# A zero-padded rotary key and regrouped SSD output products in a hybrid encoder layer on one Trainium2 core

## The chip, the cores and the metric

The kernel runs on 1 core of one Trainium2 chip. The metric is the device time of one execution in microseconds (us). Three runs of the kernel before gave a median of 2013.43 us (2013.3 to 2013.7). Below, PE is the matrix engine (TensorE) and PEld its weight load, DVE is VectorE, ACT is ScalarE, SP is the engine that issues most transfers.

## What is computed

The reference is one layer of a bidirectional encoder, 256 tokens of 2048 channels, float32 throughout:

```
n   = RMSNorm(h)
u   = n @ W_in        # MLA latents, rope key | SSD z, xBC, dt | gates
a   = MLA(u_mla)      # scores = q_nope.k_nope + q_rope.k_rope, softmax, @ v
s   = BiSSD(u_ssd)    # Mamba-2 SSD, two chunks of 128 tokens, both directions
m   = sigmoid(g_a) * a + sigmoid(g_s) * s
h   = h + m @ W_out
h   = h + ConvGatedMLP(RMSNorm(h))
out = RMSNorm_final(h)
```

Two places matter here. In the attention, 16 heads each have 128 plain channels and 64 rotary channels; the rotary key is one for all heads, so a head's scores are a product over 128 channels plus one over 64. In the SSD, 8 groups of 8 heads (64 channels a head) produce y = (own chunk's product) + (the other chunk's state, times a decay) + d * x.

## The kernel before, in words

**Precision.** Nearly every operand of a large product is split into a high part (rounded to float32r) and a low part (what is left), and a product is taken as high x high + high x low + low x high. The parts of the weights are made on the fly: `split_to` (L133) takes half a slab of 16 blocks from `raw`, ACT makes `wh` (L139) and DVE makes `wl` (L140). Five such halves are kept (HB=5), so a half that PE has finished makes room for the half five places later.

**Jobs and slots.** The work is a list of jobs, one slab of weights [128, 16 x 128] each. A job that is not merged does 48 products of 256 columns (`mm3`, L144 to L147), a merged one 16 of 512 and 16 of 256 columns (L165, L166). A job's place in the list is its slot. Work beside the weights is put into slots with `at(slot, function)` (L899) and is issued ahead of the job of that slot; a compiler's scheduler then orders each engine's instructions by that priority and by when their inputs are expected to be ready. Inside a slot PE does the side work in the order in which it is written.

**Attention.** `kr_evac` and `kr_rope` (L444 to L454, slot 14) make the rotary key once: its 64 rotated channels lie twice in 128 rows, and `krH` and `krL` are the high and the low part of all 128 rows. A rotary query `rp` (L456 to L488) has, for each head, its high part in one half of the 128 rows and its low part in the other half. `att1` (L536) makes the scores of one head, for two blocks `c` of 128 queries: three products of the plain channels, one product of `rp` with all rows of `krH` (L546, high x high and low x high at once), and one product of the 64 rows of `rp` that hold its high part with the same 64 rows of `krL` (L547). Then come the softmax on DVE and ACT (L549 to L557), transposes on PE (`att2`, L565) one slot later, and the product with the values (`att3`) another slot later. There is one `att1` for each of the 16 heads.

**SSD.** A group is 11 or 12 jobs. `ssd_xt` (L697) transposes x, `ssd_y` (L710) makes the output products, `ssd_fin` (L735) applies the gate and sums squares. `ssd_y(g, j0)` handles two of the group's four blocks `j` of 128 channels. For each block it does the products from the other chunk (L720, 128x128 weights, float32, two products that take two instructions each) and then the own chunk's products (L725, 128x64 weights, four products of two instructions, alternating between output rows 0 to 63 and 64 to 127). It is called at slot e for j0 = 0 and at slot e + 1 for j0 = 2, where e is the first slot of the next group (L1011, L1012). DVE then does L728, L731 (twice) and L733 for each call.

PSUM for side work is a pool of four banks (`spsum`, L79); each call of `ssd_y` takes two of them, `ssd_xt` two, `ssd_cb` one. Pages of SBUF come from one pool of 29 (`page`, L70), smaller tiles from one of 18 (`p1`, L73).

```
        at(b + 8 + f, ssd_xt, g)
        at(b + e, ssd_y, g, 0)
        at(b + e + 1, ssd_y, g, 2)
        at(b + e + 2, ssd_fin, g, 0)
        at(b + e + 3, ssd_fin, g, 2)
```

Of the kernel before, what the change touches and what calls it, by code (L numbers as in the profile page):

```python
# [9 lines left out]
F32R = mybir.dt.float32r  # L10
# [15 lines left out]
# columns of the packed per-channel vectors: [128, n] each  # L26
# [7 lines left out]
# columns of the shape-only constants  # L34
# [3 lines left out]
# 2 pi and the parts of a turn that 2^12 and 2^22 radians leave, as parts whose products are exact  # L38
# and a last one
# [4 lines left out]
# blocks of the SSD gate's columns of w_in that go between each group's (x and z, after z)  # L44
# [3 lines left out]
class Job:  # L48
    """One pass of a slab of weights [128, nb * 128] over the tensor engine."""
# [8 lines left out]
def tile_bidir_hybrid_layer(ctx: ExitStack, tc, xT, pos, vec, cst, w_in, w_r, w_v, w_qk, w_oa,  # L58
# [26 lines left out]
    # ---- inputs that everything needs  # L85
# [21 lines left out]
    # ---- the stream of weights: raw (DMA) -> high part (ACT) -> low part (DVE)  # L107
# [4 lines left out]
    def load(i):  # L112
        if i >= len(jobs) or i in raws:
            return
        j = jobs[i]
        t = wp.tile([P, 16, P], F32, tag="raw", bufs=RAWB, name="raw")
        raws[i] = t
        if i == 0:
            # the first slab comes in halves, between the pieces of x
            for h in range(2):  # L120
                load_x(2 * h)
                nc.sync.dma_start(t[:, 8 * h:8 * h + 8, :], j.src[:, 8 * h:8 * h + 8, :])
                load_x(2 * h + 1)
        elif i == 1:
            for h in range(2):
                nc.sync.dma_start(t[:, 8 * h:8 * h + 8, :], j.src[:, 8 * h:8 * h + 8, :])
        else:
            nc.sync.dma_start(t[:, :j.nb, :], j.src)
# [20 lines left out]
    def dense(src, nb, get, evac, cell=None, k0=0, ktot=None, merge=True):  # L149
        """One block of 128 output channels; get(k) -> [128, 2, 256], high and low activations.  # L150

        With merge, the two products of the high weights are one matmul of 512 columns, and the
        block comes as two halves that evac adds up."""
        cell = {} if cell is None else cell
        ktot = nb if ktot is None else ktot

        def mm(h, n, wh, wl):
            if k0 == 0 and h == 0:
                cell["ps"] = gpsum([P, 2, S] if merge else [P, S])
            ps = cell["ps"]  # L160
            for b in range(n):
                k = k0 + 8 * h + b
                x = get(k)
                if merge:
                    pe.matmul(ps, lhsT=wh[:, b, :], rhs=x, start=k == 0, stop=False)  # L165
                    pe.matmul(ps[:, 0, :], lhsT=wl[:, b, :], rhs=x[:, 0, :], start=False, stop=k == ktot - 1)  # L166
                else:
                    mm3(ps, wh[:, b, :], wl[:, b, :], x[:, 0, :], x[:, 1, :], k == 0, k == ktot - 1)

        def ev():  # L170
            if k0 + nb == ktot:
                evac(cell["ps"])
        j = Job(src, nb, mm, ev)
        jobs.append(j)
        return j
# [12 lines left out]
    def token_sums(accs):  # L188
        """Sums over the channels of what is in accs, one token a partition: two [128, 1] in PSUM."""
        ss = [spsum([P, 1]), spsum([P, 1])]  # L190
        for i, a in enumerate(accs):
            for c in range(2):
                pe.matmul(ss[c], lhsT=a[:, c * P:(c + 1) * P], rhs=ones[:, :1], start=i == 0,
                          stop=i == len(accs) - 1)
        return ss
# [8 lines left out]
    def spread(r):  # L204
        """[128 tokens, 2] -> [128, 256] in PSUM: the token's value on every partition."""
        dg = p1((P, 2, P), name="dg")
        ps = spsum([P, S])
        for c in range(2):
            dve.tensor_scalar(dg[:, c, :], ident, r[:, c:c + 1], None, ALU.mult)
            pe.matmul(ps[:, c * P:(c + 1) * P], lhsT=ones, rhs=dg[:, c, :], start=True, stop=True)  # L210
        return ps
# [7 lines left out]
    # ---- n = RMSNorm(x), split. The latents, which are normalised themselves, start from x * w.  # L219
# [41 lines left out]
    # ---- rotary tables  # L261
    rot = {}

    def rope_tables():
        """A step of one instruction at a time."""
# [23 lines left out]
        # angle = a + 2^12 q + 2^22 qh, all three exact; the last two as a part t of a turn  # L289
# [23 lines left out]
    def swapped(q, nb):  # L313
        """q with the two halves of 32 channels of every head swapped."""
        sw = page([P, nb, S], name="sw")
        for i in range(4):
            o = 32 * (i ^ 1)
            nc.scalar.dma_start(sw[o:o + 32], q[32 * i:32 * i + 32])
        return sw

    def rotate(q, sw, nb):
        """q, sw [128, nb, 256]: blocks of two heads of 64 channels; the rotated ones end up in q."""
# [4 lines left out]
    # ---- latents  # L327
# [14 lines left out]
    def lat_norm(which):  # L342
        # the latent is r_x * t: its mean square is r_x^2 * mean(t^2)
# [21 lines left out]
    # ---- dt, decays  # L365
# [45 lines left out]
    def dt_cumsum():  # L411
# [3 lines left out]
        for c in range(2):  # L415
            pe.matmul(ps[:, c, :64], lhsT=U, rhs=at[:, c, :64], start=True, stop=True)
            pe.matmul(ps[:, c, 64:], lhsT=L, rhs=at[:, c, 64:], start=True, stop=True)
            # the sum over the chunk that the other one is reached through
# [21 lines left out]
    # ---- MLA  # L440
# [8 lines left out]
    def kr_rope():  # L449
        t, sw = dts["krf"]  # L450
        rotate(t, sw, 1)
        kr[0], kr[1] = p1(dt=F32R, name="krH"), p1(dt=F32R, name="krL")
        act.activation(kr[0], t[:, 0, :], AF.Copy)
        dve.tensor_sub(kr[1], t[:, 0, :], f32(kr[0]))  # L454

    def r_job(i):  # L456
# [17 lines left out]
        def ro():  # L474
            for h in range(2):
                q, sw = cell["f", h]
                rotate(q, sw, 2)
                # a head's high and low parts, stacked: [high; low] for the first of a block's
                # two heads, [low; high] for the second
# [56 lines left out]
    def att1(h):  # L536
# [3 lines left out]
        rb, ro = (h // 2) % 2, 64 * (h % 2)  # L540
        ps = spsum([P, 2, S])
        for c in range(2):
            cs = slice(c * P, (c + 1) * P)
            mm3(ps[:, c, :], q[:, 0, b, cs], q[:, 1, b, cs], k[:, 0, b, :], k[:, 1, b, :], True, False)
            # the rotated key lies twice in kr: one matmul takes its high part with both parts of q
            pe.matmul(ps[:, c, :], lhsT=r[:, b, rb, cs], rhs=kr[0], start=False, stop=False)  # L546
            pe.matmul(ps[:, c, :], lhsT=r[ro:ro + 64, b, rb, cs], rhs=kr[1][ro:ro + 64, :], start=False, stop=True)  # L547
# [36 lines left out]
    # gates as tanh(u / 2); sigmoid(u) * y = (tanh(u / 2) + 1) * y / 2, the half comes with w_out  # L584
# [23 lines left out]
    # ---- SSD  # L608
# [46 lines left out]
    def ssd_decay(g, c):  # L655
# [4 lines left out]
        # decay from the chunk's edge, two heads of 64 channels a block  # L660
# [49 lines left out]
    def ssd_y(g, j0):  # L710
        q = grp[g]
        if j0 == 0:
            ypg[g] = page([P, 4, S], name="y")
        px, ps = spsum([P, 2, S]), spsum([P, 2, S])
        for b in range(2):
            j = j0 + b
            js = slice(j * P, (j + 1) * P)
            for c in range(2):
                # from the other chunk: forward into chunk 1, backward into chunk 0
                pe.matmul(px[:, b, c * P:(c + 1) * P], lhsT=q.xw[:, 1 - c, js], rhs=q.cX[:, 1 - c, :],  # L720
                          start=True, stop=True)
            for c in range(2):
                for hh in range(2):
                    h = 2 * j + hh
                    pe.matmul(ps[64 * hh:64 * hh + 64, b, c * P:(c + 1) * P],  # L725
                              lhsT=q.xt[:, c, h * 64:h * 64 + 64], rhs=q.F[c][:, h, :], start=True, stop=True)
        t = page([P, 2, S], name="yx")
        dve.tensor_mul(t, px, q.pr[:, j0:j0 + 2, :])  # L728
        y = ypg[g][:, j0:j0 + 2, :]
        for b in range(2):  # L730
            dve.scalar_tensor_tensor(y[:, b, :], q.x[:, j0 + b, :], vcol("dsk", 4 * g + j0 + b), ps[:, b, :],  # L731
                                     ALU.mult, ALU.add)
        dve.tensor_add(y, y, t)  # L733
# [54 lines left out]
    # ---- h = x + mixed @ w_out  # L788
# [34 lines left out]
    # ---- FFN  # L823
# [33 lines left out]
    def dn_evac(m, last):  # L857
        def ev(ps):
# [6 lines left out]
            if last:  # L865
# [5 lines left out]
                if m == 2:  # L871
                    # brings in the table that the last norm takes its root from
# [16 lines left out]
    # ---- the order of the work  # L889
# [7 lines left out]
    late = []          # (slot, function): work beside the slabs, in the slot in which it is issued  # L897
# [39 lines left out]
    # closures that look at state (lat) when they run, so build these jobs lazily  # L937
# [53 lines left out]
    for g in range(G):  # L991
# [19 lines left out]
        at(b + e, ssd_y, g, 0)  # L1011
        at(b + e + 1, ssd_y, g, 2)  # L1012
# [34 lines left out]
    # ---- run it  # L1047
# [4 lines left out]
    # the first slab goes through the tensor engine as float32: it needs no parts of its operands  # L1052
# [16 lines left out]
    # the tensor engine's clock comes up while the first data is on its way  # L1069
# [39 lines left out]
def _blocks(w, cols):  # L1109
    """[K, N] -> [len(cols) / 128, 128, K / 128, 128]: one contiguous slab per 128 columns."""  # L1110
# [5 lines left out]
def _layout(inp):  # L1116
# [39 lines left out]
    # rotary queries: [2, 128, block of 2 heads, k, 128]  # L1156
    a["w_r"] = uq[:, :, :, 128:].reshape(4, P, 2, 4, 128).transpose(2, 1, 3, 0, 4).reshape(2, P, 16, P)
    # values: [4, 128, k, 4 heads * 128]
    a["w_v"] = ukv[:, :, :, 128:].reshape(4, P, 4, 512).transpose(2, 1, 0, 3).reshape(4, P, 16, P)
    # per pair of heads: 2 blocks of queries, 2 of keys, [8, 128, block, k, 128]  # L1160
# [32 lines left out]
```

## Time and profile before

| | |
|---|---|
| Device time, median of 3 runs | 2013.43 us (2013.3 to 2013.7) |
| Span of the profiled execution, first to last instruction | 2011.6 us |
| The profiled execution's own time | not noted apart from the runs; 1.8 us lie between its span and the median |
| PE busy / PEld busy | 1997.7 us (99%) / 1813.1 us (90%) |
| DVE busy / ACT busy | 1477.0 us (73%) / 1187.5 us (59%) |
| Granted PE clock, mean | 0.998 of full speed |
| HBM, mean over the span | 187 GB/s |

The profile is of one execution. Matrix products are pipelined, so the duration of one (some 280 ns for 256 columns) overlaps the next; what a product costs in a stream is the step from its start to the next one's. The view of the chain that ended last gives these steps directly: each piece in it begins where the piece before it ends. Its PE times lie some 0.15 us behind those of the timeline.

### The profile page before, as it was taken

The numbers are of one execution on the slowest core, as the hardware profiler recorded it, in microseconds if no ns is written. First come the engines' busy times: TensorE is split into PE (matmuls) and PEld (weight loads), VectorE is DVE, ScalarE is ACT, GpSimd is POOL, SyncE is SP. The second block draws the span as 40 slices with busy tenths as digits, with TensorE's granted clock in tenths as the row PEclk, the third lists the DMA queues.
The fourth block names the chain that finished last, engine by engine and source line by source line (L and its number), as shares of the span: only waits on it lengthen the run. The fifth ranks groups of instructions, "written<-read, shape, count | busy, mean of one in ns | idle before, by whom it ended". The sixth has DMA issues, their size and how long they took to land.

```text
span 2011.6 us, 32781 instructions
## 1 busy us (share of the span) xinstructions
PE 1997.7 (99%) x13204; PEld 1813.1 (90%) x13204; DVE 1477.0 (73%) x2371; ACT 1187.5 (59%) x1880; POOL 0.2 (0%) x4
## 2 busy tenths in 40 slices
PE   9999999999999999999999999999999999999997
PEld 8988888999999999999888888888888888888886
DVE  7977656678778877877766666788756777567775
ACT  6655544677877877776644445655434555335564
POOL 0000000000000000000000000000000000000000
PEclk9999999999999999999999999999999999999999
DMA  7444345764556455554555555555555555555543
GB/s 273 173 170 142 130 156 207 252 215 167 193 207 224 160 203 210 176 199 174 189 203 201 201 215 194 183 192 192 185 183 187 187 189 188 188 187 183 184 164 121
DMA packets 58424, 379.54 MB, mean 189 GB/s; under 512 B 6816, under 2 KB 7456, under 8 KB 17568
## 3 DMA queue, kind: packets, MB, share of 16 engines
q1 hardware_dynamic: 56592, 375.08, 52.6%
q10 hardware_dynamic: 1680, 2.37, 0.4%
q8 instruction: 103, 1.69, 0.3%
q14 instruction: 49, 0.40, 0.1%
HBM read 371.91 MB, written 4.33 MB: 187 GB/s over the span
## 4 chain that ended last, share of the span: by engine, by line
PE 99%; DVE 1%; DMA 0%; ACT 0%; SPq 0%; DVEq 0%; issue 0%
PE g L165 41%; PE g L166 21%; PE g L145 10%; PE g L147 10%; PE g L146 10%; PE s L725 1%; PE s L720 1%; PE s L145 1%; PE s L547 0%; PE s L147 0%; PE s L146 0%; PE g L504 0%; PE g L506 0%; PE g L505 0%; PE s L704 0%; PE s L565 0%
## 5 line engine op out<-in xcount | busy, mean ns | idle before, releaser
L139 ACT ACTIVATE wh<-raw 128x1024 fp32r<-128x1024 f32 (+1 forms) x670 | 701.8, 1048 | 717.2 <-PE g L165 558.6
L140 DVE TENSOR_TENSOR wl<-raw,wh 128x1024 fp32r<-128x1024 f32 (+1 forms) x670 | 809.7, 1211 | 417.4 <-ACT wh L139 410.2
L165 PE MATMUL g<-hHL,wh 128*128 128x512 f32 x1360 | 477.6, 396 | 0.0
L145 PE MATMUL g<-xHL,wh 128*128 128x256 f32 x1424 | 405.6, 285 | 0.0
L147 PE MATMUL g<-xHL,wl 128*128 128x256 f32 x1424 | 403.1, 283 | 0.9 <-DVE wl L140 0.9
L146 PE MATMUL g<-xHL,wh 128*128 128x256 f32 x1424 | 403.0, 283 | 0.0
L166 PE MATMUL g<-hHL,wl 128*128 128x256 f32 x1360 | 381.7, 281 | 0.0
L165 PEld LDWEIGHTS g<-hHL,wh 128*128 128x128 f32 x1360 | 255.2, 188 | 60.7
L145 PEld LDWEIGHTS g<-xHL,wh 128*128 128x128 f32 x1424 | 272.3, 191 | 2.9 <-issue 2.2
L147 PEld LDWEIGHTS g<-xHL,wl 128*128 128x128 f32 x1424 | 272.3, 191 | 1.1 <-DVE wl L140 1.1
L146 PEld LDWEIGHTS g<-xHL,wh 128*128 128x128 f32 x1424 | 272.4, 191 | 0.1
L166 PEld LDWEIGHTS g<-hHL,wl 128*128 128x128 f32 x1360 | 257.1, 189 | 0.0
L165 PE MATMUL g<-aHL,wh 128*128 128x512 f32 x692 | 244.8, 399 | 0.0
L166 PE MATMUL g<-aHL,wl 128*128 128x256 f32 x692 | 193.9, 281 | 0.0
L165 PE MATMUL g<-xHL,wh 128*128 128x512 f32 x512 | 182.6, 400 | 0.0
L165 PE MATMUL g<-yHL,wh 128*128 128x512 f32 x480 | 166.5, 394 | 0.0
L165 PEld LDWEIGHTS g<-aHL,wh 128*128 128x128 f32 x692 | 130.1, 188 | 32.7 <-DVE aHL L849 0.6
L166 PE MATMUL g<-xHL,wl 128*128 128x256 f32 x512 | 143.5, 280 | 0.0
L166 PE MATMUL g<-yHL,wl 128*128 128x256 f32 x480 | 133.0, 277 | 0.0
L166 PEld LDWEIGHTS g<-aHL,wl 128*128 128x128 f32 x692 | 130.8, 189 | 0.1
L165 PEld LDWEIGHTS g<-xHL,wh 128*128 128x128 f32 x512 | 96.2, 188 | 23.4 <-issue 0.3
L165 PEld LDWEIGHTS g<-yHL,wh 128*128 128x128 f32 x480 | 90.1, 188 | 20.9
(295 smaller groups left out, 2742.4 us busy)
## 6 DMA issues: line engine op xcount, KB each, us to landing
raw<-in_w_in SPq DMA_DIRECT2D x120, 1024.0 KB, 4.8
raw<-in_w_up SPq DMA_DIRECT2D x88, 1024.0 KB, 4.8
raw<-in_w_os SPq DMA_DIRECT2D x32, 1024.0 KB, 4.8
raw<-in_w_dn SPq DMA_DIRECT2D x32, 1024.0 KB, 4.9
raw<-in_w_oa SPq DMA_DIRECT2D x16, 1024.0 KB, 4.8
FB<-acsD SPq DMA_DIRECT2D x32, 512.0 KB, 7.5
raw<-in_w_out SPq DMA_DIRECT2D x16, 1024.0 KB, 4.7
raw<-in_w_dn SPq DMA_DIRECT2D x16, 768.0 KB, 4.1
```

The lines of the kernel that those rows point to most:

```text
L139: act.activation(wh[:, :nb, :], r, AF.Copy)
L140: dve.tensor_sub(wl[:, :nb, :], r, f32(wh[:, :nb, :]))
L145: pe.matmul(ps, lhsT=wH, rhs=xH, start=first, stop=False)
L146: pe.matmul(ps, lhsT=wH, rhs=xL, start=False, stop=False)
L147: pe.matmul(ps, lhsT=wL, rhs=xH, start=False, stop=last)
L165: pe.matmul(ps, lhsT=wh[:, b, :], rhs=x, start=k == 0, stop=False)
L166: pe.matmul(ps[:, 0, :], lhsT=wl[:, b, :], rhs=x[:, 0, :], start=False, stop=k == ktot - 1)
L720: pe.matmul(px[:, b, c * P:(c + 1) * P], lhsT=q.xw[:, 1 - c, js], rhs=q.cX[:, 1 - c, :], start=True, stop=True)
L725: pe.matmul(ps[64 * hh:64 * hh + 64, b, c * P:(c + 1) * P], lhsT=q.xt[:, c, h * 64:h * 64 + 64], rhs=q.F[c][:, h, :], start=True, stop=True)
```

## The change

The rotary key's low part becomes two tiles, one for each head of a pair. In each, 64 rows hold the low part and the other 64 rows are zeros, so that the last product of a head's scores takes all 128 rows of `rp` and of the key. In the SSD, the two calls of `ssd_y` for a group become one call at slot e + 1, which issues the other chunk's products of the first two blocks, the own chunk's products of all four blocks, and the other chunk's products of the last two; the DVE work of both halves follows. Comments were taken out as well.

```diff
 def kr_rope():
     rotate(t, sw, 1)
-    kr[0], kr[1] = p1(dt=F32R, name="krH"), p1(dt=F32R, name="krL")
-    act.activation(kr[0], t[:, 0, :], AF.Copy)
-    dve.tensor_sub(kr[1], t[:, 0, :], f32(kr[0]))
+    kr["h"] = p1(dt=F32R, name="krH")
+    act.activation(kr["h"], t[:, 0, :], AF.Copy)
+    for b in range(2):
+        z = kr[b] = p1(dt=F32R, name="krL")
+        r, o = slice(64 * b, 64 * b + 64), slice(64 - 64 * b, 128 - 64 * b)
+        dve.memset(f32(z[o]), 0.0)
+        dve.tensor_sub(z[r], t[r, 0, :], f32(kr["h"][r]))
...
 def att1(h):
-    rb, ro = (h // 2) % 2, 64 * (h % 2)
+    rb = (h // 2) % 2
...
-        pe.matmul(ps[:, c, :], lhsT=r[:, b, rb, cs], rhs=kr[0], start=False, stop=False)
-        pe.matmul(ps[:, c, :], lhsT=r[ro:ro + 64, b, rb, cs], rhs=kr[1][ro:ro + 64, :], start=False, stop=True)
+        pe.matmul(ps[:, c, :], lhsT=r[:, b, rb, cs], rhs=kr["h"], start=False, stop=False)
+        pe.matmul(ps[:, c, :], lhsT=r[:, b, rb, cs], rhs=kr[b], start=False, stop=True)
...
-def ssd_y(g, j0):
+def ssd_y(g):
     q = grp[g]
-    if j0 == 0:
-        ypg[g] = page([P, 4, S], name="y")
-    px, ps = spsum([P, 2, S]), spsum([P, 2, S])
...
+    ypg[g] = page([P, 4, S], name="y")
+    px, ps = {}, {}
+    def cross(j0):
+        px[j0] = spsum([P, 2, S])
+        for b in range(2):
+            js = slice((j0 + b) * P, (j0 + b + 1) * P)
+            for c in range(2):
+                pe.matmul(px[j0][:, b, c * P:(c + 1) * P], lhsT=q.xw[:, 1 - c, js], rhs=q.cX[:, 1 - c, :],
+                          start=True, stop=True)
+    def own(j0):
+        ps[j0] = spsum([P, 2, S])
+        for b in range(2):
+            for c in range(2):
+                for hh in range(2):
+                    h = 2 * (j0 + b) + hh
+                    pe.matmul(ps[j0][64 * hh:64 * hh + 64, b, c * P:(c + 1) * P],
+                              lhsT=q.xt[:, c, h * 64:h * 64 + 64], rhs=q.F[c][:, h, :], start=True, stop=True)
+    cross(0)
+    own(0)
+    own(2)
+    cross(2)
+    for j0 in (0, 2):
+        t = page([P, 2, S], name="yx")
+        dve.tensor_mul(t, px[j0], q.pr[:, j0:j0 + 2, :])
         ...
...
-        at(b + e, ssd_y, g, 0)
-        at(b + e + 1, ssd_y, g, 2)
+        at(b + e + 1, ssd_y, g)
```

## Rows read from the trace of the kernel before

**Rows 1.** The profile's page: span, busy time, the chain that ended last

```profile
span 2011.6 us, 32781 instructions
...
PE 1997.7 (99%) x13204; PEld 1813.1 (90%) x13204; DVE 1477.0 (73%) x2371; ACT 1187.5 (59%) x1880; POOL 0.2 (0%) x4
...
PE 99%; DVE 1%; DMA 0%; ACT 0%; SPq 0%; DVEq 0%; issue 0%
```

**Rows 2.** PE's waits, longest in total first: us, times, longest

```profile
PE g L1056 <- DVE xw L225: 1.6, 3, 1.2
```

**Rows 3.** Groups by shape: PE in attention and SSD (busy, mean ns)

```profile
L547 PE MATMUL s<-krL,rp 64*128 64x256 f32 x32 | 12.2, 381 | 0.0
...
L725 PE MATMUL s<-FB,xt 128*64 128x128 f32 x256 | 21.1, 285 | 0.0
```

**Rows 4.** The chain that ended last, 116 to 119 us: start, us

```profile
116.96 0.12 PE s L546
117.08 0.31 PE s L547
117.39 0.31 PE s L145
117.71 0.12 PE s L146
```

**Rows 5.** The same chain around one call of ssd_y, 446 to 450 us

```profile
447.02 0.45 PE s L720 x4
447.47 0.59 PE s L725 x8
448.06 0.64 PE s L720 x4
448.70 0.59 PE s L725 x8
449.29 0.32 PE g L145
```

**Rows 6.** The same chain, single pieces inside that call

```profile
447.47 0.25 PE s L725
...
447.73 0.10 PE s L725
...
448.06 0.31 PE s L720
```

**Rows 7.** The same chain at a transpose of x, 434 to 436 us

```profile
434.63 0.88 PE s L704 x8
435.51 0.12 PE g L145
```

**Rows 8.** Line L546: its weight loads (duration ns min/median/max, first and last start)

```profile
L546 PEld LDWEIGHTS s<-krH,rp x32: 187/188/192, 116.7 to 259.9; 128*128 128x128 f32 x32
```

**Rows 9.** Timeline, 131 to 134 us: one head's softmax and its transposes

```profile
131.99 0.62 DVE L557 TENSOR_SCALAR p<-p,sm 128x256 f32<-128x256 f32 x2
...
132.73 0.60 PE L565 MATMUL s<-CT,p 128*128 128x128 f32 x4
```

**Rows 10.** Timeline, 103 to 106 us: the rotary key's low part and what follows

```profile
103.24 0.42 DVE L454 TENSOR_TENSOR krL<-krf,krH 128x256 fp32r<-128x256 f32 x1
103.58 2.35 DVE L140 TENSOR_TENSOR wl<-raw,wh 128x1024 fp32r<-128x1024 f32 x2
...
105.27 0.28 PE L147 MATMUL g<-latH,wl 128*128 128x256 f32 x1
```

**Rows 11.** Groups by shape: DVE's memset and its work for ssd_y

```profile
L731 DVE SCALAR_TENSOR_TENSOR y<-xs,V,s 128x256 f32<-128x256 f32 x32 | 14.4, 471 | 0.0
...
L728 DVE TENSOR_TENSOR yx<-s,pr 128x512 f32<-128x512 f32 x16 | 11.0, 686 | 1.0 <-PE s L720 0.6
...
L733 DVE TENSOR_TENSOR y<-y,yx 128x512 f32<-128x512 f32 x16 | 11.0, 686 | 0.2
...
L97 DVE MEMSET ones<- 128x128 f32 x1 | 0.2, 165 | 0.8 <-PEq L1182 0.8
```

**Rows 12.** ACT's longest wait, 400 to 960 us: us, times, longest

```profile
ACT wh L139 <- PE g L146: 94.1, 64, 2.2
```

More of the change, by code (lines that the diff above doesn't have):

```diff
@@ L708, in ssd_xt @@
                               wsuf[:, c, 8 * g:8 * g + 8].unsqueeze(2).broadcast_to([P, 8, 64]), ALU.mult)
-    def ssd_y(g, j0):
+    def ssd_y(g):
         q = grp[g]
-        if j0 == 0:
-            ypg[g] = page([P, 4, S], name="y")
-        px, ps = spsum([P, 2, S]), spsum([P, 2, S])
[L715 to L733, printed above, removed]
@@ L735, in ssd_fin @@
+        cross(0)
[5 more added lines that the diff above has]
+            dve.tensor_mul(t, px[j0], q.pr[:, j0:j0 + 2, :])
+            y = ypg[g][:, j0:j0 + 2, :]
+            for b in range(2):
+                dve.scalar_tensor_tensor(y[:, b, :], q.x[:, j0 + b, :], vcol("dsk", 4 * g + j0 + b),
+                                         ps[j0][:, b, :], ALU.mult, ALU.add)
+            dve.tensor_add(y, y, t)
     def ssd_fin(g, j0):
```

## The prediction

> **What bounds the kernel now.** I read the page first. PE is busy for 99% of the span, and the chain of work that ended last is 99% PE [rows 1]. PE's own list of waits confirms it: the largest of its five entries is 1.6 us, at the start of the kernel [rows 2]. So a microsecond taken from PE's stream comes off the end, unless something else becomes late. A busy PE hides how long a product really takes, since durations overlap (the 32 products of L547 average 381 ns [rows 3]), so I went to the chain, where each piece is a step in PE's stream. There the reader sees what the change is about. Products of one shape follow each other at 0.12 us for 256 columns. The 64-row product takes a step of 0.31, and so does the full product behind it, after which the step is 0.12 again [rows 4]. The same shows around the 64-column products of the SSD [rows 5, 6].
>
> **The padded key (attention).** Per block of queries the 64-row product costs 0.31 - 0.12 = 0.19 us more than its full twin L546 one row above, and the product after it another 0.31 - 0.12 = 0.19 [rows 4]. Padding adds no product and no column: the same 256 columns run through 128 rows, behind a product of the same shape, with the same stationary operand. I take 0.12 for it and 0.12 for the next. The group has 32 such products [rows 3], 16 heads of two blocks, and each is followed by a full-height product (the next block's or the next job's). Saved: 32 x 0.38 = **12.2 us**. As for bounds, the new product can hardly step below 0.12, the step of its twin; if it kept its 0.31 and only the return got free, 6.1 us would be saved. I take the upper end, since the row of the twin is an exact match in shape, columns and type.
>
> A rule speaks against padding. In the rows the 64-row product runs alone, and no other product shares its step [rows 4]. The Trainium skill, TensorEngine Tiling (Array Packing), section Theoretical Speedup, says that a contraction of 64 or less can run two to the array, up to twice as fast, which padding forgoes. By that price, estimated as half of a 0.12 step each, padding would cost 32 x 0.06 = 1.9 us where I count a gain. Nothing in this trace runs so, since both products of a head use the same 64 rows.
>
> **The key's preparation.** `kr_rope` loses one subtract of 128 rows (a 0.34 us step on DVE, 103.24 to 103.58 [rows 10]) and gets two of 64 rows and two memsets of 64 rows x 256. No row shows these. If half the rows cost half, the subtracts add nothing; if rows are free, they add 0.34. A memset of 128x128 took 0.165 us [rows 11]; twice the columns give at most 0.33. So 0.3 to 1.0 us more on DVE, once. Behind it in DVE's queue is the low part of the next half slab, ready near 103.58 + 1.2 = 104.8 (half of the 2.35 for two), and PE needs it at 105.27 [rows 10]. The cover is 0.5 us, so PE waits between 0 (or the memsets, which depend on nothing, go earlier) and 0.5. I take **0.3 us lost**. The half after that has another 2.9 us, 24 products at 0.12.
>
> **The SSD products.** Before, each of a group's four blocks goes 128x128, 128x64 and back. Entering: the first pair of 64-column instructions (two output halves side by side) takes 0.25, later pairs start 0.11 apart (0.25 + 3 x 0.11 makes the 0.59), so entering costs 0.14 [rows 5, 6]. Returning: the first L720 after it takes 0.31, against 0.45 / 4 = 0.11 in the call's first four; a dense product takes 0.32 against 0.12 [rows 5]. That is 0.20 either way, and 0.34 for entering and returning. After, a group does this once instead of four times: 3 x 0.34 x 8 groups = **8.2 us saved**. Adding the whole block up instead: before 2 x (0.45 + 0.59 + 0.64 + 0.59 + 0.20) = 4.94 us a group; after 0.90 for eight full ones, 0.25 + 15 x 0.11 for the 32 small ones, 0.31 + 7 x 0.11 for the last eight, 3.88. That gives 1.06 x 8 = 8.5, so the term is good to 0.3.
>
> Two steps inside the new block are not in the trace. A float32 product of full shape now stands right before the float32r dense ones; the nearest row, the float32 transposes of L704, shows no charge for that (0.12 behind them [rows 7]), the far one is the 0.20 above, so 0 to 1.6 us in all; I take 0. And the small products go from one PSUM bank to the next in mid-stream: 0 to 0.14 each, 1.1 us in all; I take 0, as pairs already alternate between output halves freely.
>
> **What is moved.** The j0 = 0 half goes one slot later, past the next group's first decay work on ACT and DVE. It issues no DMA; nothing on SP's or POOL's queue changes place. Its eight full and sixteen small instructions stay on PE. On DVE, two sets of 0.69 + 2 x 0.47 + 0.69 = 2.3 us (added durations) now come together, 4.6 us [rows 11]. Queued behind them are low parts of weights. Their cover: through the SSD, ACT waits for PE to free a weight buffer [rows 12], so the five halves are full; four halves of 24 x 0.12 = 2.9 us lie between, 11.5 us, less some 2.4 for the two splits of the refill, leaving 9. The burst fits twice. The block takes all four PSUM banks; their former users finished three slots earlier and the next one comes three slots later, at about 5.8 us a slot. `ssd_fin` of the first half now waits for the later block, but its sums are wanted only after the last group.
>
> A faster attention could make the softmax late. The closest head ends its scaling at 131.99 + 0.62 = 132.61, and PE transposes it at 132.73 [rows 9], 0.1 us of slack. But the PE work between that head's scores and its transposes is dense and untouched, so both sides move together; I charge nothing and keep 1 to 2 us for the range.
>
> **Sum.** 2011.6 - 12.2 - 8.2 + 0.3 = 1991.5 us of span [rows 1]. The profiled execution's own time is not noted apart; with the 1.8 us by which its span lies under the median of the runs, 2013.4 - 20.1 = **1993.3 us**. With the three unknown steps at their far ends it is 1996.2; with no stall and 8.5 for the SSD 1992.7. Scheduling shifts either way make this case's own range 1991.5 to 1996.
>
> **Rivals.** *The grouping does not come about.* The order on PE comes from a scheduler; if it puts dense products or the crossing ones between the small ones, the SSD term goes: 2013.4 - 12.2 + 0.3 = 2001.5. For: one more thing must be ready at once, four banks. Against: in rows 5 PE follows the code exactly, and so it does in all 16 calls in the chain. Chance 0.07.
>
> *The new product's weight load shows.* A load takes 0.188 us [rows 8], longer than a 0.12 step, so it is already under the product before it. If the padded one could not load under its twin, its step would be about 0.19 + 0.11 = 0.30, and only the return is saved, 32 x 0.19 = 6.1: 2013.4 - 6.1 - 8.2 + 0.3 = 1999.4. Against: L546 itself, a full-height load behind full-height products, steps at 0.12 [rows 4]. Chance 0.03. The Trainium skill, TensorE: Matmul & The Clock Gate, section The mechanism, says that a load overlaps running products only when its row group differs, which would give this case; the trace disagrees, by that 0.12.
>
> *The queues shift.* With new timings a softmax exponent or a page of SBUF lands behind something that waits for PE, for 0.3 us or so in some 16 heads and 8 groups: 3 to 10 us back, 1996 to 2003. For: the 0.1 us slack [rows 9] and the second `yx` page held at once. Chance 0.07.
>
> *Slower.* The DVE burst reaches PE: low parts of weights queue behind 4.6 us of output work in each group. It decides once PE stands over 20.1 / 8 = 2.5 us per group; with no lead at all it would be 8 x 4.6 = 36.8, or 2030 us. Against: the 9 us lead. Chance 0.03.
>
> **How the numbers follow.** The forecast case has 0.80. The range 1991 to 1998.5 holds it nearly whole and the near part of the queue case. A measurement of this kernel tells 0.2%, 4 us, from no change. All cases but the last are faster by more than that, save a corner of the queue case: faster 0.96, same 0.01, slower 0.03.
>
> **What would show it.** Right: in the chain the last product of `att1` and the one behind it step 0.12; a group's SSD block is one piece of 8, 32 and 8 instructions of about 3.9 us, with one 0.25 and one 0.31 in it and 0.12 behind it; PE's list of waits grows by less than 1 us; L547's group has the 128x128 shape. Wrong: L547 still at 0.3, several entries into the 128x64 shape per group, or PE waiting for `wl`, `p` or a PSUM bank in the middle of the kernel.

## The result and the profile after

The changed kernel took 1994.13 us (median of 4 runs, 1992.78 to 1994.73) against 2013.37 us: ratio 0.9906, 95% interval 0.9894 to 0.9918. The forecast was 1993.3 us. In a second comparison it took 1993.54 us (5 runs, 1992.60 to 1993.90) against 2013.14, ratio 0.9903 (0.9889 to 0.9917). The profiled execution is the slowest of the first four, 1994.73 us with a span of 1992.9, so 18.7 us of span are gone in it.

The page after, the same parts as in [rows 1]:

```profile
span 1992.9 us, 32794 instructions
...
PE 1979.4 (99%) x13204; PEld 1810.8 (91%) x13204; DVE 1471.3 (74%) x2374; ACT 1205.5 (60%) x1894; POOL 0.2 (0%) x4
...
PE 97%; DVE 2%; DMA 0%; ACT 0%; issue 0%; ACTq 0%; SPq 0%; DVEq 0%
```

PE is still busy for 99%, with the same 13204 instructions, so the gain is not work left out. The chain that ended last is 97% PE and no longer 99%: at one wait of PE near 106 us, explained below, it is followed back through DVE. The groups by shape (compare [rows 3]) show the low part's product at 128x128; L727 and L736 are now the lines of the crossing and the own products:

```profile
L727 PE MATMUL s<-cX,xw 128*128 128x128 f32 x128 | 17.7, 282 | 0.0
L736 PE MATMUL s<-FB,xt 128*64 128x128 f32 x256 | 15.7, 276 | 0.0
...
L552 PE MATMUL s<-krL,rp 128*128 128x256 f32 x32 | 9.0, 282 | 0.0
```

The chain that ended last, in one head's scores (start, length; compare [rows 4]):

```profile
117.96 0.12 PE s L551
118.07 0.12 PE s L552
118.19 0.12 PE s L145
```

And at a group's output products (compare [rows 5]):

```profile
441.70 0.89 PE s L727 x8
442.60 1.90 PE s L736 x32
444.49 1.09 PE s L727 x8
445.58 0.12 PE g L145
```

The low part's product and the product behind it have lost their 0.31. The SSD block is 3.88 us in one piece, and the dense product behind it steps 0.12.

**Where the time went.** The same marks in the chain of both kernels cut the span into stages: the last product before the attention's preparation, the transposes of the first and of the last head, and the sums after the last group. Before:

```profile
67.37 0.54 PE s L210 x4
...
124.31 0.44 PE s L565 x4
...
267.13 0.44 PE s L565 x4
...
979.54 0.79 PE s L193 x8
```

After:

```profile
67.50 0.54 PE s L210 x4
...
124.55 0.44 PE s L570 x4
...
256.05 0.44 PE s L570 x4
...
960.38 0.79 PE s L193 x8
```

| stage | before, us | after, us | saved |
|---|---|---|---|
| start to 67 us | 67.37 | 67.50 | -0.13 |
| to the first head's transposes (two low-part products) | 56.94 | 57.05 | -0.11 |
| to the last head's (30 of them) | 142.82 | 131.50 | 11.32 |
| to the sums after the SSD (8 groups) | 712.41 | 704.33 | 8.08 |
| to the end of the span | 1032.06 | 1032.52 | -0.46 |

The sum is 18.7. The two middle stages pay nearly what the forecast gave them. The second stage should have gained 0.76 (two times 0.38) and lost 0.11, so something there costs 0.87 us. PE's list of waits names it; its largest entry is now the low part of a weight half (total us, times, longest):

```profile
PE g L147 <- DVE wl L140: 1.5, 2, 0.9
```

One of the two is the 0.9 us at the start, as before. The other is in the timeline at 106 us (compare [rows 10]; DVE first, then PE):

```profile
102.93 0.42 DVE L179 TENSOR_TENSOR gate<-gate,g 128x256 f32<-128x256 f32 x1
103.46 0.27 DVE L458 MEMSET krL<- 64x256 f32 x1
103.75 0.42 DVE L459 TENSOR_TENSOR krL<-krf,krH 64x256 fp32r<-64x256 f32 x1
104.17 0.27 DVE L458 MEMSET krL<- 64x256 f32 x1
104.45 0.42 DVE L459 TENSOR_TENSOR krL<-krf,krH 64x256 fp32r<-64x256 f32 x1
104.89 2.36 DVE L140 TENSOR_TENSOR wl<-raw,wh 128x1024 fp32r<-128x1024 f32 x2
...
105.27 0.28 PE L146 MATMUL g<-latL,wh 128*128 128x256 f32 x1
106.17 0.39 PE L147 MATMUL g<-latH,wl 128*128 128x256 f32 x1 [0.61 <-DVE wl L140]
106.39 0.28 PE L145 MATMUL g<-latH,wh 128*128 128x256 f32 x1
```

The weight half that PE needs next stands behind four instructions for the padded key. It starts 1.31 us later than in [rows 10], and PE stands for it. The list counts this wait from the end of the product before, 0.61 us. By starts it is the whole 0.87: L147 begins 0.90 us behind L146 and the next product 0.22 behind L147, where both steps are 0.12 otherwise.

### The profile page after: what moved, and what is told of

It reads as the page before. It is cut to its first block, busy times and chain, and to the rows that moved or that the text cites. A ratio compares the mean times of both kernels' runs of the same rounds, so it can differ in the third digit from the quotient of the medians.

```text
span 1992.9 us, 32794 instructions
## 1 busy us (share of the span) xinstructions
PE 1979.4 (99%) x13204; PEld 1810.8 (91%) x13204; DVE 1471.3 (74%) x2374; ACT 1205.5 (60%) x1894; POOL 0.2 (0%) x4
## 4 chain that ended last, share of the span: by engine, by line
PE 97%; DVE 2%; DMA 0%; ACT 0%; issue 0%; ACTq 0%; SPq 0%; DVEq 0%
PE g L165 41%; PE g L166 21%; PE g L147 10%; PE g L146 10%; PE g L145 10%; PE s L727 1%; PE s L736 1%; PE s L147 0%; PE s L145 0%; PE s L146 0%; DVE wl L140 0%; PE s L709 0%; PE s L570 0%; DVE xHL L232 0%; DMA x<-in_xT 0%; PE g L509 0%
## 5 line engine op out<-in xcount | busy, mean ns | idle before, releaser
L147 PE MATMUL g<-xHL,wl 128*128 128x256 f32 x1424 | 403.5, 283 | 0.9 <-DVE wl L140 0.9
L146 PE MATMUL g<-xHL,wh 128*128 128x256 f32 x1424 | 403.6, 283 | 0.2 <-DVE xHL L232 0.2
L147 PEld LDWEIGHTS g<-xHL,wl 128*128 128x128 f32 x1424 | 272.1, 191 | 1.1 <-DVE wl L140 1.1
L146 PEld LDWEIGHTS g<-xHL,wh 128*128 128x128 f32 x1424 | 272.2, 191 | 0.4 <-DVE xHL L232 0.4
```

The costliest lines, as they stand in the source:

```text
L146: pe.matmul(ps, lhsT=wH, rhs=xL, start=False, stop=False)
L147: pe.matmul(ps, lhsT=wL, rhs=xH, start=False, stop=last)
```

## The experiments

Each is compared with the kernel before on the same chip. The first four ran together (before: 2012.90 us, 7 runs), the last four together (before: 2013.14 us, 14 runs).

**Each part alone.** First the padded key with the old SSD:

```diff
-        at(b + e + 1, ssd_y, g)
+        at(b + e, ssd_y, g, 0)
+        at(b + e + 1, ssd_y, g, 2)
```

(with the old `ssd_y`). Expected:

> The padded key alone, with the SSD output products as before. If a change of shape and back costs 0.38 us in the attention, 32 of them are gone: 12.2 us, less the 0.9 us for which PE stood at the first keys in the changed kernel's trace: 2013.4 - 12.2 + 0.9 = 2002.1 us. If padding is worth nothing and the grouping made the whole gain, about 2014 us. In the chain the last product of the scores and the one behind it step 0.12 us each; the SSD blocks look as before (0.45, 0.59, 0.64, 0.59).

Measured: 2001.59 us (4 runs, 2001.38 to 2001.69), ratio 0.9943 (0.9927 to 0.9960), 11.3 us saved.

Then the grouping with the old key:

```diff
-            pe.matmul(ps[:, c, :], lhsT=r[:, b, rb, cs], rhs=kr[b], start=False, stop=True)
+            pe.matmul(ps[:, c, :], lhsT=r[ro:ro + 64, b, rb, cs], rhs=kr[1][ro:ro + 64, :], start=False, stop=True)
```

(with the old `kr_rope`). Expected:

> The grouped SSD products alone, with the 64-row product as before. By the changed kernel's chain a group takes 3.88 us in place of 4.94, so 8 x 1.06 = 8.5 us: 2013.4 - 8.5 = 2004.9 us, and no wait of PE at 106 us. If the two parts are not independent (one hides a part of the other), this and the run of the padding alone don't add up to the 19.2 us of the whole change: their gains would differ from it by over 1.5 us.

Measured: 2004.60 us (4 runs, 2003.91 to 2005.01), ratio 0.9958 (0.9943 to 0.9973), 8.3 us saved. The two gains make 19.6 us; the whole change gave 19.2 and 19.6 in its two comparisons. So the parts add up within 0.4 us, and neither hides a part of the other that these runs can tell. Their stages agree with the table: from the first to the last head's transposes 131.50 us with the padding alone and 142.81 with the grouping alone; in the SSD stage 712.41 and 704.34.

**Is the 64-row product slow, or the passage to it?** In the kernel before each 64-row product has a passage of its own, so the two can't be told apart there. This kernel keeps 64 rows, but puts a head's two next to each other:

```diff
+            low = lambda: pe.matmul(ps[:, c, :], lhsT=r[ro:ro + 64, b, rb, cs], rhs=kr[1][ro:ro + 64, :],
+                                    start=c == 1, stop=c == 0)
+            if c == 1:
+                low()
-            mm3(ps[:, c, :], ..., True, False)
+            mm3(ps[:, c, :], ..., c == 0, False)
...
+            if c == 0:
+                low()
```

Expected:

> The grouped SSD as in the changed kernel; the low part is unpadded and multiplied with 64 rows as before, but a head's two 64-row products stand next to each other (last of the first block, first of the second). If what costs is the change of shape, there is one passage a head in place of two: 16 x 0.38 = 6.1 us are saved against two passages, 6.1 us less than padding saves, and no wait at 106 us: 1994.1 + 6.1 - 0.9 = 1999.3 us; the second 64-row product steps 0.12 us. If a 64-row product is slow in itself (0.31 us), only the return is saved, 16 x 0.19 = 3.0: 2002.4 us, and both step 0.31 us.

Measured: 1998.78 us (4 runs, 1998.55 to 1998.92), ratio 0.9929 (0.9915 to 0.9944). Its chain at the second head's scores, L544 being the two 64-row products and L549 the one with all rows:

```profile
124.33 0.12 PE s L549
124.45 0.43 PE s L544 x2
124.88 0.31 PE s L145
125.19 0.12 PE s L146
```

Two of them take 0.43, that is 0.31 and 0.12, and the product behind them takes 0.31 once. So the passage from one shape to the other costs, not the 64 rows. The time fits one passage a head (1999.3) and not a slow product (2002.4): against the grouping alone, in the same comparison, it is 5.8 us less, 0.36 for each of 16 passages. The stage from the first head to the last took 136.70 us, 6.12 under before, where 15 passages of 0.38 make 5.7; the 0.4 beyond that is not explained.

What a passage spends its time on, no experiment shows. The weight loads (PEld) suggest an answer. In the kernel before, around the first 64-row product:

```profile
116.68 0.19 PEld L546 LDWEIGHTS s<-krH,rp 128*128 128x128 f32 x1
116.80 0.28 PE L546 MATMUL s<-krH,rp 128*128 128x256 f32 x1
117.01 0.18 PEld L547 LDWEIGHTS s<-krL,rp 64*128 64x128 f32 x1
117.01 0.38 PE L547 MATMUL s<-krL,rp 64*128 64x256 f32 x1
117.32 0.19 PEld L145 LDWEIGHTS s<-qk 128*128 128x128 f32 x1
117.32 0.38 PE L145 MATMUL s<-qk 128*128 128x256 f32 x1
```

The load of L546 starts 0.12 us ahead of its product; those of L547 and of the product behind it start together with theirs. And the price of each way is close to the length of the load on the far side: 0.19 against 0.183 us (64 rows) and 0.19 against 0.188 in the attention, 0.14 against 0.137 (64 columns) and 0.20 against 0.192 in the SSD. A load that can't run ahead across a passage would give these prices. That is a reading that fits and not a cause shown: no run holds the shape and changes the load.

**Do passages cost the same in the SSD, when there are more of them?** The block stays in its slot, but each pair of own products stands behind its crossing product:

```diff
-        cross(0)
-        own(0)
-        own(2)
-        cross(2)
+        for j0 in (0, 2):
+            px[j0], ps[j0] = spsum([P, 2, S]), spsum([P, 2, S])
+            for b in range(2):
...
+                for c in range(2):
+                    pe.matmul(px[j0][:, b, c * P:(c + 1) * P], ...)
+                    for hh in range(2):
+                        pe.matmul(ps[j0][64 * hh:64 * hh + 64, b, c * P:(c + 1) * P], ...)
```

Expected:

> The padded key as in the changed kernel; the SSD output products of a group still come in one block of slot e + 1, but each pair of own products stands right behind its crossing product, so that a group goes into the 128x64 shape and back 8 times instead of once. If the passage is what costs, at 0.34 us: 7 x 0.34 x 8 = 19.0 us more than the changed kernel, 1994.1 + 19.0 = 2013.1 us, and the block takes about 6.3 us in place of 3.9. If the grouping gained by having one call in place of two, or by moving VectorE's work to one slot, the time stays within 1 us of 1994.1.

Measured: 2011.89 us (10 runs, 2011.75 to 2013.28), ratio 0.9995 (0.9986 to 1.0005): 18.4 us slower than the changed kernel in the same comparison, 1993.54. With eight passages a group, where the kernel before has four, nearly the whole gain is given back, the padding's too. Its chain (L730 own, L726 crossing):

```profile
441.15 0.37 PE s L730 x4
441.52 0.42 PE s L726 x2
441.94 0.37 PE s L730 x4
```

Four small instructions take 0.37 (0.25 and 0.11), two crossing ones 0.42 (0.31 and 0.11). The SSD stage took 723.68 us against 704.33; 19.35 over 56 further passages is 0.346 us each. Against the kernel before it is 11.27 us longer (712.41) with 32 further passages, 0.352 each. The price is the same whether the other kernel has one call a group or two, so that it is one call, in one slot, is worth nothing by itself within 0.2 us.

**What are the 0.9 us lost before the attention?** First without zeros. The key's low part lies in both halves anyway, so all its rows can be used as they are:

```diff
-            pe.matmul(ps[:, c, :], lhsT=r[:, b, rb, cs], rhs=kr[b], start=False, stop=True)
+            pe.matmul(ps[:, c, :], lhsT=r[:, b, rb, cs], rhs=kr[1], start=False, stop=True)
```

(with the old `kr_rope` and its `krH`). Expected in its first run:

> The grouped SSD as in the changed kernel, and the last product of the scores takes all 128 rows of the query and of the key's low part, which lies in both halves anyway: no zeros, one subtract as before. It adds the product low x low, which neither kernel has. If the 0.9 us wait of PE near 106 us comes from the four VectorE instructions for the padded key ahead of a weight half, it is gone, and the time is 0.9 us under the changed kernel's: 1993.2 us. If the wait has another cause (the new schedule), it stays: 1994.1 us. The steps in the scores stay at 0.12 us in either case, unless zeros in half of the rows matter to PE.

Measured: 1992.99 us (4 runs, 1992.78 to 1994.26), ratio 0.9902 (0.9887 to 0.9917). The changed kernel's own comparison, 1994.13 of 2013.37, was on another occasion, and the two ranges overlap, so this time alone shows little. The trace shows more: no wait at that place, and 56.18 us from 67 us to the first head's transposes, 0.87 under the changed kernel. From the first head to the last it takes 131.50 us, as with zeros, so the gain comes from the full height and not from the zeros. Both kernels and one in between were then run together. The one in between only issues the zeros earlier:

```diff
+    def kr_zero():
+        for b in range(2):
+            z = kr[b] = p1(dt=F32R, name="krL")
+            o = slice(64 - 64 * b, 128 - 64 * b)
+            dve.memset(f32(z[o]), 0.0)
...
+    at(12, kr_zero)
     at(14, kr_rope)
```

Expected with the zeros early:

> The changed kernel with the two memsets of the padded key two slots earlier (slot 12), so that only the two subtracts stand before the weight half near 106 us. If the wait of PE there is the length of VectorE's queue against a cover of 0.5 us, the queue is about 0.6 us shorter than in the changed kernel, and of the 0.9 us lost some 0.3 are left: 0.6 us under the changed kernel of the same call. If the wait has another cause it stays, and so does the time.

Expected of the changed kernel, run once more:

> The changed kernel again, for comparison with the two others of this call that differ from it in VectorE's instructions for the key alone: 1994.1 us, with a wait of PE of 0.6 us near 106 us; the last four products for the final norm may step more slowly or not, since the granted clock falls while PE is idle there (0.5 us in its first profile).

Expected without zeros, run once more:

> The version without zeros once more, on the same chip as the changed kernel: 0.9 us under it if the wait near 106 us is the whole difference, so about 1993.2 us; equal within 0.3 us if the difference of the first two comparisons was chance.

Measured:

| kernel | median, us (range; runs) | DVE steps for krL, us | 67 us to first transposes |
|---|---|---|---|
| changed kernel | 1993.54 (1992.60 to 1993.90; 5) | four, 1.43 | 56.93 |
| zeros early | 1992.74 (1991.68 to 1993.24; 4) | two, 0.86 | 56.21 |
| no zeros | 1992.65 (1991.88 to 1993.17; 4) | one, 0.34 | 56.19 |

The timeline of the kernel with early zeros, DVE and then PE:

```profile
102.23 0.42 DVE L179 TENSOR_TENSOR gate<-gate,g 128x256 f32<-128x256 f32 x1
102.57 0.84 DVE L464 TENSOR_TENSOR krL<-krf,krH 64x256 fp32r<-64x256 f32 x2
103.43 2.36 DVE L140 TENSOR_TENSOR wl<-raw,wh 128x1024 fp32r<-128x1024 f32 x2
...
104.77 0.33 PE L147 MATMUL g<-latH,wl 128*128 128x256 f32 x1
```

With one instruction before the weight half PE has time to spare. With two the half comes just as PE wants it: the product is a little longer, and 0.03 us is lost. With four PE stands, 0.74 to 0.75 us for the changed kernel in this comparison and 0.87 in the first. So the wait is the length of DVE's queue at that point beyond a cover: 0.5 us more is free, 1.3 us more is not. The expectation of 0.3 us left with early zeros was too high: it took the queue to be 0.6 us shorter, and from the `gate` instruction to the weight half it was 0.76 (1.20 in place of 1.96). The times lie in this order too, but 0.9 us is less than the 0.2% (4 us) that times alone can tell from no change. By what the traces show, the two versions are better than the changed kernel by 0.7 to 0.9 us. The version without zeros multiplies low x low in addition.

## Why the prediction was right, and where not

**PE's stream sets the end.** Right. The stages' savings are PE's steps. In PE's list of waits only the one at 106 us and one of 0.2 us in the first 67 us are new.

**The padded key, 12.2 us.** Right. From the first head's transposes to the last one's 11.32 us were saved for 30 products, 0.377 each, and two more lie before. All 32 make 12.1. The new product steps 0.12, at the upper end that was taken.

*The new product's weight load shows.* It did not: L552 follows L551 at 0.12. The Trainium skill, TensorE: Matmul & The Clock Gate, section The mechanism, says in one sentence that a load overlaps running products only when its row group differs, and in another that a load into the background weight buffer runs ahead too. The trace disagrees with the first, by that 0.12, and agrees with the second.

The runs price a change of shape here at 0.19 us going in and 0.19 coming back, and a second product of the same shape at nothing more than its 0.12. The Trainium skill, TensorEngine Tiling (Array Packing), section Key Properties, says that a change of the tiling mode, and not just of the tile, drains TensorE. The runs agree with it in where the cost lies: the two neighbouring 64-row products take 0.31 and 0.12, and the SSD's small products, which alternate between two halves of the output, go on at 0.11 a pair.

**The SSD products, 8.2 us.** Right: 8.08 by the stage, 8.3 by the part alone. The block has the 3.88 us that were added up; the sum by blocks, 8.5, was 0.4 more than the stage shows. Both unknown steps inside it were taken at 0 by the nearest row, and neither cost anything. The dense product behind a float32 product of full shape steps 0.12, and the 32 own products take 1.90, which is 0.25 and fifteen times 0.11, so the change of PSUM bank is free.

**The key's preparation, 0.3 us: the step that failed in size.** The mechanism was as put: four DVE instructions before the weight half, 0.5 us of cover, PE waits for the rest. The estimate was 0.3 to 1.0 us more on DVE; it was 1.28. The memsets of 64 rows took 0.27 us and stepped 0.29 and 0.28, inside their bound of 0.33. Two things went over. The bound let two subtracts of 64 rows step 0.34 each at most, as the one of 128 rows did; they stepped 0.42 and 0.44, so they added 0.52 in place of 0.34 at most. And the first memset started 0.53 us behind the instruction before it, where the subtract had started at 0.34: another 0.19, for which the prediction had no term. The 0.5 us stall that was taken as the far end thus became 0.75 to 0.87 in the changed kernel, where 0.3 had been forecast.

**The DVE burst (the slower rival), the queues and the grouping.** None of them came. PE waits nowhere in the SSD. ACT still waits for PE to free weight buffers there, which is the cover that was named (compare [rows 12]):

```profile
ACT wh L139 <- PE g L146: 77.4, 67, 1.9
```

The scheduler kept the written order in all eight blocks. The softmax with 0.1 us of slack made no wait: PE's list has none between the first and the last head. The same head's scaling now ends at 132.06, and its transposes start at 132.20.

**The sum.** Forecast were 20.1 us less; the span of the profiled execution is 18.7 shorter. The savings of 12.1 and 8.1 less the wait of 0.9 make 19.3. Another 0.13 us were lost before 67 us and 0.46 after the SSD, and neither belongs to a term of the prediction. The medians, 19.2 and 19.6 us less, lie a little nearer.

## What to carry to other kernels

Where PE is the bound, as here, look in the chain for products whose step is longer than a twin's of the same columns, and at their neighbours: here one 64-row product between full ones cost 0.38 us, half of it in the product behind it. Either give the odd product the common shape, if the other half's data or zeros can fill it, or put all products of one shape next to each other; count passages, not products. And when a side job grows by a few small instructions, look for what stands next in that engine's queue and how long before its use it is done: here 0.5 us more was free and 1.3 us more was not.

## What was not expected

**A 64-row subtract takes as long as a 128-row one, and its neighbours did not overlap it.** Both take 0.42 us for 256 columns. The 128-row one starts 0.34 us behind the instruction before it and the next one 0.34 behind it, so they overlap by 0.08. With the early zeros the first 64-row subtract, on rows 0 to 63, also starts 0.34 behind; but the second, on rows 64 to 127, and the weight half behind it, which starts at row 0, each start only when the one before has ended (0.84 for the two, and 0.02). So the change of the first row may cost here and not the number of rows. It is not shown: in the changed kernel the second memset has the rows of the subtract before it and does not overlap it either.

**The end of the kernel varies with PE's clock.** After the last dense product PE waits twice, for 0.6 and 0.9 us. The four products of the final norm (L210) follow, in a stretch whose granted clock differs between executions. Two stretches of 2 us around them, before and after:

```profile
2000.60:2002.60 2.00, 1.13 (x8) 1.02 (x8) 0.65 (x3) 0.88 (x3) 0.00 (x0) 1.00 0.00 0
```

```profile
1981.90:1983.90 2.00, 1.13 (x6) 0.99 (x5) 0.65 (x3) 0.45 (x3) 0.00 (x0) 0.62 0.00 0
```

The seventh figure is the mean granted clock, 1.00 (2.4 GHz) and 0.62 (part of the stretch at 1.2 GHz). The four products take 0.73 us and 1.24. That is the 0.5 us in the last row of the table of stages. The changed kernel's second profile has 0.72 us for them, and the ten profiles of this case have 0.72 to 1.24. So it belongs to the execution and not to the change, and can explain some 0.5 us of the spread, up to 2 us, among runs of one kernel.
